# An HGRN2 and ConvFFN layer on one core: the modulation's column loads issued from GpSimd's queue

## The chip, the cores and the metric

One core of a Trainium2 chip runs the whole layer. The metric is the time of one execution on the device in microseconds (us). Engines are named by what they do and, in the rows, by the profile's short names: TensorE (PE; PEld for its weight loads), VectorE (DVE), ScalarE (ACT), GpSimd (POOL), SyncE (SP). Each runs its own queue of instructions strictly in order. A transfer (DMA) is issued from a queue, too, and waits there until what it overwrites has been read.

## The reference

One layer for 256 latent tokens (x) and 256 context tokens (ctx), 2048 wide, fp32. A vector c gives six rows of modulation for the latents (c_ctx for the context): shift, scale and gate of the mixer, shift, scale and gate of the FFN.

```
m = silu(c) @ ada_w + ada_b                 # (2048) x (2048 x 6*2048); parts 0 to 5
h = norm(x) * (1 + m[1]) + m[0]             # the context with silu(c_ctx)
y = hgrn2(h_latent, h_context)              # 16 heads: q, f, b, v, g = h @ w_in; gated recurrence, both ways
x = x + m[2] * norm(y)
h = norm(x) * (1 + m[4]) + m[3]
f = (silu(conv3(h @ w_gate)) * (h @ w_up)) @ ffn_w_out
out = x + m[5] * norm(f)
```

## The kernel before

Every weight comes from HBM as fp32, as a tile w_raw of 512 KB (L133, four buffers), and is split into a high and a low half: ScalarE casts w_hi (L108), VectorE subtracts and writes w_lo (L109). TensorE then makes three matmuls of each product (mm3, L212 to L214: high with high, high with low, low with high). w_hi and w_lo have three buffers; the casts run up to two tiles ahead (`LOOK`). A w_raw buffer is free for the next load when w_lo has been written.

The program runs in stages: the start (all tokens normalised; the first four heads, weights taken in rows of w_in), the projection of the heads in pairs p = 2 to 7 with the recurrence of earlier pairs (`scan`) laid between their matmuls, the mixer's output product, the FFN's input products (22 blocks), the FFN's output product.

Parts 0 and 1 of the modulation are made on TensorE at the start. Parts 2 to 5 are made by `ada_part` (L355), one column block at a time: a tile ada_w of 128 rows by 512 columns (256 KB) is loaded (L359), and VectorE multiplies it by a column of c and adds it up into ada_acc (L374 for the first of 16, L376 for the rest; here called *sums*). A part has 4 blocks of 16 tiles, so 64 loads and 64 sums; TensorE then adds the 128 partitions with a matrix of ones (L385). `loaded` is called ahead: ada_w has four buffers (`ADA_BUFS`), in part 5 five (`GATE_BUFS`), and each new load waits for the sum that read its buffer. Parts 2 to 4 are stepped along with the projection (`ada_rest`, `step`), part 5 along with the FFN's blocks. Parts 2 and 5 end with two memsets on GpSimd (L406), for the bias and the gain.

The order on each engine isn't written out: a scheduler puts the instructions into the queues by the program's priorities and by its own model of what is ready when. The weights' preparation has a raised priority (L138). SyncE's queue holds all loads, the weights' and these.

In `scan`, the output of a pair is squared on ScalarE (L843), VectorE makes 1/sqrt in small steps (`rsqrt`, L78 to L83), ScalarE scales by it (L850), and TensorE transposes the result (L858).

Of the kernel before, what the change touches and what calls it, by code (L numbers as in the profile page):

```python
# [17 lines left out]
P = 128  # L18
D = 2048
# [18 lines left out]
def tile_hgrn2_convffn_layer(  # L38
# [4 lines left out]
    nc = tc.nc  # L43
    V, S, PE = nc.vector, nc.scalar, nc.tensor
    x, ctx_in, out = x[0], ctx_in[0], out[0]
    ada_w, ada_b = ada_w[0], ada_b[0]
# [23 lines left out]
    def bank(pool, name):  # L70
        return pool.tile([P, 512], F32, name=name)
# [283 lines left out]
    def ada_part(part, pool, bufs=ADA_BUFS):  # L355
        def loaded(i):
            b, r = divmod(i, KT)
            aw = pool.tile([P, 512], F32, name="ada_w", bufs=bufs)
            nc.sync.dma_start(out=aw, in_=ada_w[r * P:(r + 1) * P, part * D + b * 512:part * D + (b + 1) * 512])  # L359
            return aw  # L360

        accs = []
        aws = [loaded(i) for i in range(bufs - 1)]
        yield
        yield
        for b in range(4):
            acc = pool.tile([P, 512], F32, name="ada_acc", bufs=4)
            for r in range(KT):

                if len(aws) < 4 * KT:  # L370
                    aws.append(loaded(len(aws)))
                aw = aws[b * KT + r]
                if r == 0:
                    V.tensor_scalar(out=acc, in0=aw, scalar1=c_cols[:, r:r + 1], scalar2=None, op0=ALU.mult)  # L374
                else:
                    V.scalar_tensor_tensor(out=acc, in0=aw, scalar=c_cols[:, r:r + 1], in1=acc,  # L376
                                           op0=ALU.mult, op1=ALU.add)
                yield
            accs.append(acc)
        for _ in range(8):  # L380
            yield

        one = bank(ps_mi, "mi")
        for b in range(4):
            PE.matmul(out=one[32 * b:32 * b + 32, :], lhsT=ones32, rhs=accs[b], start=True, stop=True,  # L385
                      tile_position=(0, 32 * b), skip_group_check=True)
        strip_sb = pool.tile([P, 512], F32, name="ada_w", bufs=bufs)
        S.copy(out=strip_sb, in_=one)
        for _ in range(4):
            yield  # L390
        if part in (3, 4):
            tp = bank(ps_mi, "mi")
            for i in range(4):
                PE.transpose(out=tp[:, i * P:(i + 1) * P], in_=strip_sb[:, i * P:(i + 1) * P], identity=ident)
            dst = shc_f if part == 3 else scc_f

            V.tensor_tensor(out=dst.rearrange("p (b i) -> p i b", i=4),
                            in0=tp.rearrange("p (i b r) -> p i b r", i=4, r=32)[:, :, :, 0],
                            in1=adab[:, part, :].rearrange("p (b i) -> p i b", i=4), op=ALU.add)
            if part == 4:  # L400
                V.scalar_tensor_tensor(out=scc_f, in0=scc_f, scalar=1.0, in1=g_ffn, op0=ALU.add, op1=ALU.mult)
        else:
            post = n_mix_post if part == 2 else n_ffn_post
            for w, src in enumerate((ada_b[part * D:(part + 1) * D], post[0])):
                gb = pool.tile([P, 512], F32, name="ada_acc", bufs=4)
                nc.gpsimd.memset(gb, 0.0)  # L406
                nc.sync.dma_start(out=gb[0::32, :], in_=src.rearrange("(b n) -> b n", b=4))
                V.tensor_tensor(out=strip_sb, in0=strip_sb, in1=gb, op=(ALU.add, ALU.mult)[w])
            gd = dram.tile([4, 512], F32, name=f"gd{part}")
            nc.sync.dma_start(out=gd, in_=strip_sb[0::32, :])  # L410
            grow[part] = gd
        yield
# [755 lines left out]
```

## Time and profile before

| | |
|---|---|
| median of 3 runs | 1739.77 us (1739.51 to 1744.2) |
| the profiled execution | 1737.13 us, its span 1735.4 us, mean granted clock 0.996 |
| TensorE busy | 1688.0 us (97%) |
| VectorE busy | 1154.8 us (67%) |
| ScalarE busy | 772.9 us (45%) |
| GpSimd busy | 3.4 us |
| read from HBM | 348 MB, 202 GB/s over the span |
| loads of ada_w | 256 of 256 KB, from SyncE's queue, median 4.1 us to landing |

The span runs from the first to the last instruction; the execution's own time lies 1.7 us around it. Busy time is a union: overlapping matmuls count once. A row of waiting names the instruction that waited, what ended the wait, the total in us, how often, and the longest. Issuing a transfer isn't counted as busy time.

### The profile page before, as it was taken

How to read it: one execution, taken by the hardware profiler on the slowest of the kernel's cores; microseconds unless marked ns; L12 is line 12 of the kernel's file. 1: busy time of each engine (PE TensorE's matmuls, PEld its weight loads, DVE VectorE, ACT ScalarE, POOL GpSimd, SP SyncE). 2: the span in 40 equal slices, each digit the busy share in tenths (PEclk: the TensorE clock that was granted, in tenths of full speed). 3: DMA queues.
4: the chain of work that ended last, by engine and by line, in shares of the span. 5: the costliest groups of instructions: out<-in, count | busy, mean ns of one | idle time of the engine just before them, and what ended most of it. 6: DMA issues, size and time to landing. Idle time of an engine off the chain costs nothing.

```text
span 1735.4 us, 31973 instructions
## 1 busy us (share of the span) xinstructions
PE 1688.0 (97%) x12990; PEld 1506.1 (87%) x12990; DVE 1154.8 (67%) x1857; ACT 772.9 (45%) x1176; POOL 3.4 (0%) x13
## 2 busy tenths in 40 slices
PE   6999999899999999999999899999999999999998
PEld 4777888888989899888988798999999999888886
DVE  6777898855548875697565798766666666544444
ACT  4322264454544354443464644444444444443443
POOL 0000000000000000000000000000000000000000
PEclk9999999999999999999999999999999999999999
DMA  9886657633326863677357579766666666655654
GB/s 353 289 299 231 223 171 233 216 108 107 110 75 204 287 213 106 206 235 231 111 166 271 192 262 314 235 193 194 190 195 195 194 194 195 202 195 192 199 194 146
DMA packets 274646, 352.57 MB, mean 203 GB/s; under 512 B 12954, under 2 KB 197675, under 8 KB 273987
## 3 DMA queue, kind: packets, MB, share of 16 engines
q1 hardware_dynamic: 274499, 350.53, 62.1%
q8 instruction: 102, 1.67, 0.4%
q14 instruction: 45, 0.37, 0.1%
HBM read 348.37 MB, written 2.11 MB: 202 GB/s over the span
## 4 chain that ended last, share of the span: by engine, by line
PE 78%; DVE 10%; DMA 8%; issue 3%; ACT 1%; SPq 0%; DVEq 0%; ACTq 0%
PE pj L212 24%; PE pj L214 24%; PE pj L213 24%; DMA ada_w<-in_ada_w_dram 7%; DVE ada_acc L376 3%; DVE w_lo L109 2%; PE o L429 2%; DVE k L706 1%; PE sc L746 1%; PE mi L818 1%; DMA aw<-in_ada_w_dram 0%; ACT w_hi L108 0%; PE pj L347 0%; DMA w_raw<-in_hgrn_w_in_dram 0%; DVE f L709 0%
## 5 line engine op out<-in xcount | busy, mean ns | idle before, releaser
L109 DVE TENSOR_TENSOR w_lo<-w_raw,w_hi 128x1024 fp32r<-128x1024 f32 x452 | 552.9, 1224 | 393.6 <-ACT w_hi L108 389.7
L108 ACT CAST w_hi<-w_raw 128x1024 fp32r<-128x1024 f32 x452 | 473.3, 1049 | 679.0 <-PE pj L213 369.6
L214 PE MATMUL pj<-h2h,w_lo 128*128 128x256 f32 x1376 | 380.9, 277 | 5.4 <-DVE w_lo L109 5.3
L212 PE MATMUL pj<-h2h,w_hi 128*128 128x256 f32 x1376 | 380.2, 276 | 0.0
L213 PE MATMUL pj<-h2l,w_hi 128*128 128x256 f32 x1376 | 379.9, 276 | 0.0
L212 PE MATMUL pj<-hTh,w_hi 128*128 128x256 f32 (+1 forms) x1040 | 352.9, 340 | 2.7 <-ACT hTh L108 1.6
L214 PE MATMUL pj<-hTh,w_lo 128*128 128x256 f32 (+1 forms) x1040 | 347.6, 335 | 0.8 <-DVE w_lo L109 0.6
L213 PE MATMUL pj<-hTl,w_hi 128*128 128x256 f32 (+1 forms) x1040 | 347.3, 334 | 0.0
L214 PEld LDWEIGHTS pj<-h2h,w_lo 128*128 128x128 f32 x1376 | 258.3, 188 | 6.9 <-DVE w_lo L109 6.8
L212 PEld LDWEIGHTS pj<-h2h,w_hi 128*128 128x128 f32 x1376 | 258.3, 188 | 0.9 <-issue 0.8
L213 PEld LDWEIGHTS pj<-h2l,w_hi 128*128 128x128 f32 x1376 | 258.3, 188 | 0.0
L212 PEld LDWEIGHTS pj<-hTh,w_hi 128*128 128x128 f32 x1040 | 195.5, 188 | 31.1 <-issue 5.0
L214 PEld LDWEIGHTS pj<-hTh,w_lo 128*128 128x128 f32 x1040 | 195.3, 188 | 23.8 <-DVE w_lo L109 2.1
L213 PEld LDWEIGHTS pj<-hTl,w_hi 128*128 128x128 f32 x1040 | 195.7, 188 | 19.6 <-DVE hTl L109 0.2
L376 DVE SCALAR_TENSOR_TENSOR ada_acc<-ada_w,c_cols,ada_acc 128x512 f32<-128x512 f32 x240 | 179.8, 750 | 45.2 <-DMA ada_w<-in_ada_w_dram 42.0
L214 PE MATMUL pj<-w_hi,al 128*128 128x512 f32 x352 | 138.7, 394 | 0.0
L213 PE MATMUL pj<-w_lo,ah 128*128 128x512 f32 x352 | 138.0, 392 | 0.0
L212 PE MATMUL pj<-w_hi,hTh 128*128 128x256 f32 (+1 forms) x448 | 135.3, 302 | 1.5 <-DVE q L481 0.8
L212 PE MATMUL pj<-w_hi,ah 128*128 128x512 f32 x352 | 136.6, 388 | 0.0
L213 PE MATMUL pj<-w_lo,hTh 128*128 128x256 f32 (+1 forms) x448 | 133.0, 297 | 0.2 <-DVE w_lo L109 0.2
L214 PE MATMUL pj<-w_hi,hTl 128*128 128x256 f32 (+1 forms) x448 | 133.1, 297 | 0.0
L212 PEld LDWEIGHTS pj<-w_hi,hTh 128*128 128x128 f32 x448 | 85.3, 190 | 5.7 <-DVE stage L479 1.7
(227 smaller groups left out, 1792.8 us busy)
## 6 DMA issues: line engine op xcount, KB each, us to landing
w_raw<-in_ffn_w_in_dram SPq DMA_DIRECT2D x172, 512.0 KB, 3.6
w_raw<-in_hgrn_w_in_dram SPq DMA_DIRECT2D x160, 512.0 KB, 4.5
ada_w<-in_ada_w_dram SPq DMA_DIRECT2D x256, 256.0 KB, 4.1
w_raw<-in_ffn_w_out_dram SPq DMA_DIRECT2D x88, 512.0 KB, 4.0
aw<-in_ada_w_dram SPq DMA_DIRECT2D x64, 512.0 KB, 8.0
w_raw<-in_hgrn_w_out_dram SPq DMA_DIRECT2D x32, 512.0 KB, 4.3
hTh<-in_x_dram SPq DMA_DIRECT2D x2, 1024.0 KB, 4.9
hTh<-in_ctx_dram SPq DMA_DIRECT2D x2, 1024.0 KB, 10.2
```

What stands on the lines that cost most here:

```text
L108: S.copy(out=hi, in_=src)
L109: V.tensor_tensor(out=lo, in0=src, in1=hi.bitcast(F32), op=ALU.subtract)
L212: PE.matmul(out=o, lhsT=lh, rhs=rh, start=first, stop=False, skip_group_check=True)
L213: PE.matmul(out=o, lhsT=lh, rhs=rl, start=False, stop=False, skip_group_check=True)
L214: PE.matmul(out=o, lhsT=ll, rhs=rh, start=False, stop=last, skip_group_check=True)
L376: V.scalar_tensor_tensor(out=acc, in0=aw, scalar=c_cols[:, r:r + 1], in1=acc, op0=ALU.mult, op1=ALU.add)
L429: PE.matmul(out=strip[32 * a:32 * (a + 1), :], lhsT=cst[:, r4 * 4 + a, :], rhs=aws[r4][:, a].rearrange("p s n -> p (s n)"), start=(r4 == 0 ...
L706: V.tensor_tensor(out=half(t, i, m), in0=half(t, i, m), in1=half(by, 1 - i, m)[:, :, 0:1].to_broadcast([P, 256 // m, m]), op=ALU.mult)
L746: PE.matmul(out=o[32 * b:32 * b + 32, 32 * i:32 * i + 32], lhsT=flat(lhs[b % 2])[:, s0:s0 + 32], rhs=flat(rhs[b % 2])[:, t0:t0 + 32], star ...
L818: PE.matmul(out=sps[:, cs], lhsT=kT[:, d, h, ct], rhs=v[:, 2 + ct, h * P:(h + 1) * P], start=(ct == 0), stop=(ct == 1))
```

## The change

The loads of L359 are issued from GpSimd's queue. Nothing else is edited.

```
-            nc.sync.dma_start(out=aw, in_=ada_w[r * P:(r + 1) * P, part * D + b * 512:part * D + (b + 1) * 512])
+            nc.gpsimd.dma_start(out=aw, in_=ada_w[r * P:(r + 1) * P, part * D + b * 512:part * D + (b + 1) * 512])
```

The scheduler builds other orders from it. GpSimd's queue, from the end of the start on; the memsets are those of parts 2 and 5 (ident and ib are constants):

```order
 L320 IOTA ib 128x32
-L406 MEMSET ada_acc 128x512 x4
+L359 DMA ada_w<-in_ada_w_dram 128x512 x64
+L406 MEMSET ada_acc 128x512 x2
+L359 DMA ada_w<-in_ada_w_dram 128x512 x192
+L406 MEMSET ada_acc 128x512 x2
```

All 256 loads now stand there, with two memsets between the loads of part 2 and those of part 3; SyncE's queue keeps the rest in the order it had.

VectorE in part 4, from the row that ends part 3 (L397 writes shc_f) on, before:

```order
L397 TENSOR_TENSOR shc_f<-mi,colsB 128x4x4
L376 SCALAR_TENSOR_TENSOR ada_acc<-ada_w,c_cols,ada_acc 128x512 x5
L109 TENSOR_TENSOR w_lo<-w_raw,w_hi 128x1024
L376 SCALAR_TENSOR_TENSOR ada_acc<-ada_w,c_cols,ada_acc 128x512 x4
L109 TENSOR_TENSOR w_lo<-w_raw,w_hi 128x1024
L376 SCALAR_TENSOR_TENSOR ada_acc<-ada_w,c_cols,ada_acc 128x512 x5
L109 TENSOR_TENSOR w_lo<-w_raw,w_hi 128x1024
L374 TENSOR_SCALAR ada_acc<-ada_w,c_cols 128x512
L376 SCALAR_TENSOR_TENSOR ada_acc<-ada_w,c_cols,ada_acc 128x512 x2
L109 TENSOR_TENSOR w_lo<-w_raw,w_hi 128x1024
L376 SCALAR_TENSOR_TENSOR ada_acc<-ada_w,c_cols,ada_acc 128x512
L109 TENSOR_TENSOR w_lo<-w_raw,w_hi 128x1024
```

The same place now:

```order
L397 TENSOR_TENSOR shc_f<-mi,colsB 128x4x4
L376 SCALAR_TENSOR_TENSOR ada_acc<-ada_w,c_cols,ada_acc 128x512 x6
L109 TENSOR_TENSOR w_lo<-w_raw,w_hi 128x1024
L376 SCALAR_TENSOR_TENSOR ada_acc<-ada_w,c_cols,ada_acc 128x512 x5
L109 TENSOR_TENSOR w_lo<-w_raw,w_hi 128x1024
L376 SCALAR_TENSOR_TENSOR ada_acc<-ada_w,c_cols,ada_acc 128x512
L374 TENSOR_SCALAR ada_acc<-ada_w,c_cols 128x512
L376 SCALAR_TENSOR_TENSOR ada_acc<-ada_w,c_cols,ada_acc 128x512 x4
L109 TENSOR_TENSOR w_lo<-w_raw,w_hi 128x1024
L376 SCALAR_TENSOR_TENSOR ada_acc<-ada_w,c_cols,ada_acc 128x512 x2
L109 TENSOR_TENSOR w_lo<-w_raw,w_hi 128x1024
L376 SCALAR_TENSOR_TENSOR ada_acc<-ada_w,c_cols,ada_acc 128x512 x3
```

Ahead of the third w_lo stand 17 sums of this piece where 14 stood, ahead of the fifth 22 where 18 stood; one more sum has moved to just ahead of the piece.

VectorE in part 2, at the end of the rsqrt of the first pair (rs and nw_t are its tiles; L650 gates the q of pair 3 and L689 begins the next recurrence), before:

```order
L376 SCALAR_TENSOR_TENSOR ada_acc<-ada_w,c_cols,ada_acc 128x512
L109 TENSOR_TENSOR w_lo<-w_raw,w_hi 128x1024
L82 TENSOR_TENSOR nw_t_2921<-nw_t_2921,ss_2912 128x4
L376 SCALAR_TENSOR_TENSOR ada_acc<-ada_w,c_cols,ada_acc 128x512
L83 SCALAR_TENSOR_TENSOR rs_2913<-nw_t_2921,rs_2913 128x4
L109 TENSOR_TENSOR w_lo<-w_raw,w_hi 128x1024
L689 TENSOR_TENSOR tmp<-k_3128,k_3133 128x512
```

and now:

```order
L376 SCALAR_TENSOR_TENSOR ada_acc<-ada_w,c_cols,ada_acc 128x512
L109 TENSOR_TENSOR w_lo<-w_raw,w_hi 128x1024
L82 TENSOR_TENSOR nw_t_2921<-nw_t_2921,ss_2912 128x4
L650 SCALAR_TENSOR_TENSOR q<-pj,tmp 128x512
L83 SCALAR_TENSOR_TENSOR rs_2913<-nw_t_2921,rs_2913 128x4
L689 TENSOR_TENSOR tmp<-k_3128,k_3133 128x512
```

The w_lo that followed the last L83 is now ahead of it (it is the one shown), and so are L650 and, counted from the start of the burst, two more sums. On TensorE the four transposes L858 of this pair stand 22 matmuls later than before; its order is otherwise the same.

## Rows read from the trace of the kernel before

**Rows 1.** Page of the profile: span, and busy us (share) xinstructions by engine.

```profile
span 1735.4 us, 31973 instructions
...
PE 1688.0 (97%) x12990; PEld 1506.1 (87%) x12990; DVE 1154.8 (67%) x1857; ACT 772.9 (45%) x1176; POOL 3.4 (0%) x13
```

**Rows 2.** Who waited for whom, TensorE, whole run: us in total, times, longest.

```profile
PE pj L214 <- DVE w_lo L109: 5.9, 9, 1.9
PE mi L858 <- ACT tmp L850: 5.8, 2, 4.3
```

**Rows 3.** Stretches: the four bursts and one without; us, each engine's busy us (instructions), clock, DMA.

```profile
core 0: us, PE busy (x) PEld busy (x) DVE busy (x) ACT busy (x) POOL busy (x), PEclk, DMA share, GB/s
262.00:352.00 90.00, 85.23 (x900) 76.76 (x899) 79.28 (x165) 42.57 (x89) 0.00 (x0) 0.96 0.68 217
529.00:632.00 103.00, 100.90 (x878) 90.89 (x877) 91.41 (x164) 43.89 (x81) 0.00 (x0) 1.00 0.79 254
705.00:815.00 110.00, 105.17 (x901) 94.25 (x901) 90.22 (x162) 43.41 (x82) 0.00 (x0) 1.00 0.75 240
1014.00:1102.00 88.00, 82.57 (x709) 81.06 (x708) 78.91 (x103) 39.60 (x47) 0.00 (x0) 1.00 0.90 302
1115.00:1203.00 88.00, 88.00 (x778) 88.00 (x778) 54.51 (x61) 42.42 (x49) 0.00 (x0) 1.00 0.62 192
```

**Rows 4.** Tile ada_w in each burst: idle before its instructions until what; us, times.

```profile
  DMA ada_w<-in_ada_w_dram: 8.1, 7
...
  DMA ada_w<-in_ada_w_dram: 10.6, 14
...
  DMA ada_w<-in_ada_w_dram: 15.9, 13
...
  DMA ada_w<-in_ada_w_dram: 8.9, 10
```

**Rows 5.** Tile ada_w, whole run: duration ns min/median/max; landing us.

```profile
L359 SPq DMA_DIRECT2D ada_w<-in_ada_w_dram x256: 327/328/1370, 204.6 to 1091.2; - x128
...
L374 DVE TENSOR_SCALAR ada_acc<-ada_w,c_cols x16: 460/480/488, 210.6 to 1069.2; 128x512 f32<-128x512 f32 x16
...
DMA to landing us min/median/max: 2.5/4.1/6.3
```

**Rows 6.** VectorE in order of time, part 4: start us, us, instruction [idle before].

```profile
718.55 0.75 DVE L376 SCALAR_TENSOR_TENSOR ada_acc<-ada_w,c_cols,ada_acc 128x512 f32<-128x512 f32 x1 [2.67 <-DMA ada_w<-in_ada_w_dram]
...
726.45 3.12 DVE L376 SCALAR_TENSOR_TENSOR ada_acc<-ada_w,c_cols,ada_acc 128x512 f32<-128x512 f32 x4 [1.85 <-DMA ada_w<-in_ada_w_dram]
731.44 0.75 DVE L376 SCALAR_TENSOR_TENSOR ada_acc<-ada_w,c_cols,ada_acc 128x512 f32<-128x512 f32 x1 [1.87 <-DMA ada_w<-in_ada_w_dram]
732.11 1.22 DVE L109 TENSOR_TENSOR w_lo<-w_raw,w_hi 128x1024 fp32r<-128x1024 f32 x1
```

**Rows 7.** Who waited for whom, SyncE's queue, whole run.

```profile
SPq L133 <- DVE w_lo L109: 862.6, 352, 8.5
...
SPq L359 <- DVE ada_acc L376: 96.5, 142, 5.8
```

**Rows 8.** VectorE in order of time, FFN burst.

```profile
1034.02 0.75 DVE L376 SCALAR_TENSOR_TENSOR ada_acc<-ada_w,c_cols,ada_acc 128x512 f32<-128x512 f32 x1
```

**Rows 9.** SyncE's queue in order of time, FFN burst.

```profile
1038.48 0.38 SPq L133 DMA_DIRECT2D w_raw<-in_ffn_w_in_dram  x1
1038.90 0.51 SPq L359 DMA_DIRECT2D ada_w<-in_ada_w_dram  x1
```

**Rows 10.** GpSimd in order of time, around the end of part 2.

```profile
526.73 0.99 POOL L406 MEMSET ada_acc<- 128x512 f32 x2 [524.79 <-PE mi L385]
```

**Rows 11.** TensorE in order of time, part 4.

```profile
733.38 0.39 PE L214 MATMUL pj<-hTh,w_lo 128*128 128x256 f32 x1 [0.21 <-DVE w_lo L109]
```

**Rows 12.** Stretches behind TensorE's wait of 4.3 us, columns as in rows 3.

```profile
318.70:323.10 4.40, 4.40 (x21) 4.40 (x22) 3.67 (x8) 3.19 (x11) 0.00 (x0) 0.50 1.00 342
323.10:327.50 4.40, 4.40 (x41) 4.40 (x41) 3.29 (x9) 1.78 (x4) 0.00 (x0) 1.00 0.06 22
```

## Prediction

> **What bounds the kernel now.** I read the engines' busy time first, then who waits for whom, then the four stretches in which the moved loads run, and last the order of the instructions in them.
>
> TensorE is busy for 1688 us of a span of 1735.4, VectorE for 1155 [rows 1]. So whatever the change does, it can give back only what TensorE waits for, 47 us in all. Its longer waits behind VectorE's in-order queue are 5.9 us for w_lo (the low halves of the weights), and 5.8 us for the transposes of L858, which wait for ScalarE's L850, which waits for the last step of VectorE's rsqrt [rows 2].
>
> The 256 moved loads fall into four bursts of 64, one for each part: three while the pairs of heads are projected, one at the start of the FFN. In the four TensorE idles 4.8, 2.1, 4.8 and 5.4 us, VectorE 11, 12, 20 and 9; in the FFN's burst TensorE runs 709 matmuls in 88 us where the same length of time without a burst takes 778, so that burst costs 69/778 of 88 us = 7.8 us of TensorE [rows 3].
>
> VectorE's own waits in the bursts are for these loads: 7, 14, 13 and 10 of them, 8.1 to 15.9 us in each [rows 4]. A burst has four buffers (the FFN's five). A load is issued when the sum four places ahead has read its buffer, and it lands 4.1 us (median; least 2.5) after that [rows 5]. A buffer's round in the projection is thus about 0.33 issue + 4.1 landing [rows 5] + 0.78 for the sum itself (3.12 us for four [rows 6]) = 5.2 us, with the semaphores between them about 5.3, so four buffers give a sum each 1.33 us where VectorE alone would take 0.78. **The round trip of one load sets the pace of a burst**, not the bytes: the DMA engines are 75 to 79% busy in parts 3 and 4, and 90% in the FFN's burst [rows 3].
>
> Last, the queue that is relieved. SyncE's weight loads wait for VectorE's w_lo, which gives their buffer back (352 waits, 863 us), and its ada_w loads wait for the sums, 97 us [rows 7]. Neither wait is the other's fault while the pairs are projected. In the FFN it is: the sum that ends at 1034.8 (0.75 after 1034.02) frees a buffer, but the load for it is issued at 1038.90, behind a weight load that waited until 1038.48 for w_lo [rows 8, 9]. That is 4.1 us of queue. This is what the change can win.
>
> **The change, part by part.**
>
> *SyncE* loses 256 issues of 0.33 us [rows 5], 84 us of a queue that nobody is waiting on. Worth 0 by itself: its weight loads wait for VectorE's w_lo [rows 7], not for the queue. The Trainium skill, "DMA: Bandwidth & Descriptors", section "Issuing engines are not separate DMA queues", says that loads from all queues run on the same 16 engines and that a second queue saves only the issuing time. By that rule alone the sum would be 0; the traces' head-of-line wait above and VectorE's new order below are what it leaves out. It is my second case.
>
> *GpSimd* gets 256 loads and is otherwise idle. Queued on it beside them are only the four memsets of L406; the first two now stand between part 2's loads and part 3's, and take 0.99 us together at 526.7 [rows 10]. The first loads of part 3 go out some 3 us later than now, at a place where TensorE waits for no w_lo. Cost 0.
>
> *FFN burst (part 5).* Loads no longer wait behind weights: up to 4.1 us off a round. VectorE's 10 waits there are 8.9 us [rows 4], TensorE's loss 7.8. But the DMA engines are at 90% [rows 3]: of 88 us only 10% is left. Bounds 0 and -7.8. I take **-3.5**, a little under half, since the freed loads press on the same nearly full engines.
>
> *VectorE's order.* The scheduler now places the sums earlier, ahead of w_lo that TensorE is about to need. In part 4 the third w_lo after shc_f has 18 sums of the burst before it where it had 14, the fifth 23 where it had 18 (one of the extra ones stands just ahead of the piece shown). The third w_lo runs at 732.11 and TensorE is waiting for it: its matmul starts at 733.38 after a wait [rows 6, 11]. So all that is put ahead of it goes to TensorE: four sums at 0.78 (data there) to 1.33 (paced by the round trip), 3.1 to 5.3 us, up to 6.6 with the fifth's. Three waits for landings, of 2.7, 1.9 and 1.9 us, stand right ahead of it [rows 6], so I take the pace: **+5.3**. In part 2 the last rsqrt step has two more sums, one w_lo and one L650 before it: 2 x 0.78 to 2 x 1.33, plus 1.2 and some 0.6 = 3.4 to 4.5 us later. TensorE comes to the four transposes 22 matmuls of 0.107 us (4.4 / 41 [rows 12]) = 2.4 us later. Net +1.0 to +2.1, taken **+1.3**; the wait of 4.3 us stays that long, and so the clock still falls with it: after the wait TensorE runs at 0.50 (1.2 GHz) for 4.4 us, 21 matmuls where the next 4.4 us have 41 [rows 12]. In part 3 one sum more stands ahead of most w_lo: 0 where TensorE has reserve, 1.3 where not, taken **+0.6**. Sum +7.2.
>
> *The round trip.* No load in the trace is issued by GpSimd, so the change of a load's round, d, has to be bounded. From below: if a queue of its own spares a load all waiting behind weights, it lands in the least time, 2.5 instead of 4.1 [rows 5]: d = -1.6. From above: GpSimd has to make up the transfer itself, and takes 0.5 us for one pass over a tile of this shape (two in 0.99 [rows 10]); one pass for the reading and one for the writing side, against 0.33 issue, make +0.7 (2 x 0.5 - 0.33), and SyncE's slowest issue, 1.37 us [rows 5], +1.0. I take **d = +0.4**, between one pass (+0.2) and two (+0.7), and so near the upper end, because half of the waiting behind weights is not saved when two queues share the engines. The Trainium skill ("DMA: Bandwidth & Descriptors", "Latency and other measured facts") gives about 1 us to the first byte from GpSimd and 0.6 from SyncE; by that alone d would be +0.4 too, and no run here shows it yet. Of the 34 waits in parts 2 to 4 [rows 4] I count about half, 16, ahead of places where TensorE has no reserve; the rest falls into VectorE's other idle time. 16 x 0.4 = **+6.4**.
>
> Sum: -3.5 + 7.2 + 6.4 = **+10.1 us**. The profiled execution took 1737.1, so 1747.2; the runs shown have a median of 1739.8, 2.7 above it, so **1749.9 us**, 0.6% slower.
>
> **The rivals.**
>
> *No change.* GpSimd's loads land as SyncE's did, and the sums put earlier are covered by time that VectorE would have idled. For it: VectorE idles 9 to 20 us in each burst [rows 3]. Against: at the tight places it idles for these loads alone. With d = 0 the sum is 7.2 - 3.5 = +3.7, 1743.5.
>
> *Faster.* A load no longer stands behind 512 KB of weights, neither in SyncE's queue nor in the DMA engines' rings. For it: the landings of 4 to 6 us beside a least of 2.5. It decides from d about -0.6. At d = -0.8 the 16 waits give back 12.8, but in the projection TensorE has no more to give than the waits of L858 and w_lo and the slow clock behind one of them, about 4.3 + 2.2 [rows 2, 12] + 1 = 7.5; VectorE's order then costs only 0.78 a sum, 3.1 + 0.8; the FFN gives 6: -9.6, 1730.
>
> *GpSimd as the pace.* If a load takes GpSimd more than the 1.33 us of a round's quarter, the queue itself sets the bursts. At 2 us, 64 loads take 128 us where the bursts take 88 to 110 [rows 3]: some 17 us of TensorE in each of four after reserves of about 10, near 1807. The Trainium skill ("SBUF — State Buffer", "SBUF: two separate sides") describes such a trap: GpSimd cannot write a load's descriptors while VectorE holds their shared port. It names copies and single-input operations in a fast mode, and here that is 16 sums of 0.48 us [rows 5] of 256; the rest have two inputs. So I give it little.
>
> *It doesn't take effect* is excluded: GpSimd's queue holds the 256 loads in the built order.
>
> **How the numbers follow.** Forecast (d from 0.1 to 1): 0.50. No change: 0.26. Faster: 0.14. GpSimd as the pace: 0.10. About 0.3%, 5.2 us, is what a measurement of this kernel can tell from no change; the forecast and the last case lie above it, so slower 0.60, same 0.26, faster 0.14. Range: upward all terms at their worse end short of the last case, 6.6 + 2.1 + 1.3 + 0 and d = 0.7 in all 34 waits (24) = +33, 1773; downward into the faster case as far as 1735. What is left out is most of the last case and the better part of the faster one, about 0.17.
>
> **What would show it.** After: the loads stand under a second queue; the issue-to-landing median is 4.2 to 4.8 us; VectorE's waits for ada_w grow from 45 to 55 us or more; TensorE waits for w_lo near the third w_lo of part 4, several us, instead of 0.21; the FFN's burst has more than 709 matmuls in its 88 us. I am wrong if the landings come down to 3.5 us or less, if TensorE's waits for w_lo in parts 2 to 4 stay under 2 us, or if the FFN's burst gains more than 6 us.

## The result, and the profile after

| | before | changed |
|---|---|---|
| median of 3 runs | 1739.77 us | 1758.76 us (1756.33 to 1761.8) |
| ratio | | 1.0109, 95% interval 1.0091 to 1.0128 |
| span of the profiled execution | 1735.4 us | 1760.0 us |

The change costs 19.0 us, 1.1%. The forecast was +10.1 us (1749.9, range 1735 to 1773): the right side and inside the range, but little more than half the size.

The page of the changed kernel's profile, span and busy time (before: [rows 1]):

```profile
span 1760.0 us, 32088 instructions
...
PE 1699.7 (97%) x12990; PEld 1518.3 (86%) x12990; DVE 1154.8 (66%) x1857; ACT 773.1 (44%) x1176; POOL 140.7 (8%) x269
```

The 24.6 us of longer span fall in two parts. TensorE is idle for 60.3 us instead of 47.4, 12.9 more. And it is *busy* for 11.7 us more with the same 12990 matmuls: that is a lower clock, as the rows on the clock below show. VectorE's busy time is the same to the tenth, so no work was added there.

Who waited for whom, TensorE, whole run (before: [rows 2]):

```profile
PE mi L858 <- ACT tmp L850: 12.6, 2, 8.2
PE pj L214 <- DVE w_lo L109: 9.6, 7, 4.0
```

The transposes L858 wait 12.6 us instead of 5.8, the matmuls behind w_lo 9.6 instead of 5.9. The four bursts, in windows that begin and end at the same instructions of TensorE (to within a few) as those of [rows 3], and the stretch without a burst; columns as there:

```profile
263.70:359.90 96.20, 87.88 (x900) 79.26 (x899) 80.75 (x167) 42.62 (x89) 25.19 (x47) 0.95 0.65 208
537.00:649.30 112.30, 102.60 (x878) 92.18 (x877) 91.17 (x164) 43.63 (x81) 34.48 (x65) 0.95 0.77 247
722.10:840.40 118.30, 109.81 (x901) 98.84 (x900) 92.83 (x165) 46.70 (x85) 32.70 (x61) 0.96 0.70 226
1040.50:1126.60 86.10, 82.79 (x705) 81.81 (x705) 79.85 (x104) 39.95 (x46) 23.14 (x43) 0.98 0.94 314
1139.60:1227.60 88.00, 88.00 (x779) 88.00 (x778) 54.50 (x61) 42.39 (x49) 0.00 (x0) 1.00 0.63 193
```

For the same matmuls part 2 now takes 96.2 us instead of 90, part 3 112.3 instead of 103, part 4 118.3 instead of 110. The FFN's burst has 705 matmuls in 86.1 us, 720 in 88, where it had 709. Without a burst nothing changed. The clock column (PEclk) was 0.96 in part 2 and 1.00 in the other bursts; it is now between 0.95 and 0.98 in all four.

Tile ada_w, whole run: duration of the issue in ns, landing in us (before: [rows 5]):

```profile
L359 POOL DMA_DIRECT2D ada_w<-in_ada_w_dram x256: 536/536/676, 207.8 to 1107.6; - x128
...
DMA to landing us min/median/max: 2.8/3.9/6.5
```

GpSimd takes 0.54 us for a load (SyncE: 0.33), never over 0.68, and it lands 3.9 us after its issue (4.1).

Where two of the longest stalls come from can be read on VectorE and TensorE. Part 3, the rsqrt before the second L858 (the row of L844 begins it, the last L83 ends it; time, us, instruction, idle before):

```profile
612.99 0.16 DVE L844 TENSOR_SCALAR ss<-ss 128x4 f32<-128x4 f32 x1
613.11 0.75 DVE L376 SCALAR_TENSOR_TENSOR ada_acc<-ada_w,c_cols,ada_acc 128x512 f32<-128x512 f32 x1
...
616.90 0.75 DVE L376 SCALAR_TENSOR_TENSOR ada_acc<-ada_w,c_cols,ada_acc 128x512 f32<-128x512 f32 x1 [1.58 <-DMA ada_w<-in_ada_w_dram]
...
618.43 0.48 DVE L374 TENSOR_SCALAR ada_acc<-ada_w,c_cols 128x512 f32<-128x512 f32 x1
...
620.57 0.75 DVE L376 SCALAR_TENSOR_TENSOR ada_acc<-ada_w,c_cols,ada_acc 128x512 f32<-128x512 f32 x1 [1.20 <-DMA ada_w<-in_ada_w_dram]
621.24 1.22 DVE L109 TENSOR_TENSOR w_lo<-w_raw,w_hi 128x1024 fp32r<-128x1024 f32 x1
622.37 0.15 DVE L83 SCALAR_TENSOR_TENSOR rs<-nw_t,rs 128x4 f32<-128x4 f32 x1
```

The same place in the trace of before:

```profile
601.27 0.16 DVE L844 TENSOR_SCALAR ss<-ss 128x4 f32<-128x4 f32 x1
...
606.20 0.15 DVE L83 SCALAR_TENSOR_TENSOR rs<-nw_t,rs 128x4 f32<-128x4 f32 x1
```

From L844 to the end of the last L83 it took 5.1 us and now takes 9.5: one sum, an L374 and a w_lo more stand in between (0.75 + 0.48 + 1.22 = 2.4 us), and two loads are waited for (1.58 + 1.20). TensorE, in order of time, in part 3 and at the third w_lo of part 4 (there 0.21 before [rows 11]):

```profile
622.98 0.73 PE L858 MATMUL mi<-ident,tmp 128*128 128x128 f32 x2 [8.24 <-ACT tmp L850]
...
754.71 0.58 PE L214 MATMUL pj<-hTh,w_lo 128*128 128x256 f32 x1 [3.99 <-DVE w_lo L109]
```

And the clock around the first of them, two stretches of equal length (columns as in [rows 3]):

```profile
616.70:627.00 10.30, 4.02 (x12) 3.13 (x12) 8.80 (x19) 3.11 (x6) 4.28 (x8) 0.50 0.68 227
627.00:637.30 10.30, 10.30 (x46) 8.35 (x45) 7.90 (x11) 1.82 (x2) 3.75 (x7) 1.00 0.76 248
```

The clock is at its lower level, 1.2 GHz (0.50), for 10.3 us that begin within the wait, and back at 1.00 after it.

VectorE in part 4, ahead of the third w_lo, the one that TensorE waits 3.99 us for (before: [rows 6]):

```profile
735.19 2.37 DVE L376 SCALAR_TENSOR_TENSOR ada_acc<-ada_w,c_cols,ada_acc 128x512 f32<-128x512 f32 x3 [3.31 <-DMA ada_w<-in_ada_w_dram]
...
744.74 0.75 DVE L376 SCALAR_TENSOR_TENSOR ada_acc<-ada_w,c_cols,ada_acc 128x512 f32<-128x512 f32 x1 [2.09 <-DMA ada_w<-in_ada_w_dram]
...
751.98 1.54 DVE L376 SCALAR_TENSOR_TENSOR ada_acc<-ada_w,c_cols,ada_acc 128x512 f32<-128x512 f32 x2 [2.49 <-DMA ada_w<-in_ada_w_dram]
753.43 1.22 DVE L109 TENSOR_TENSOR w_lo<-w_raw,w_hi 128x1024 fp32r<-128x1024 f32 x1
```

**By stage.** For the rest of the document the loss is counted by stages: the start of the same TensorE instruction, counted from the first, in two traces, and by how much its lag grows from one end of a stage to the other. (Instructions number 1530, 2428, 3999, 4874, 5605, 6505, 7684 and 8663 start at 262, 352, 529, 632, 705, 815, 985 and 1115 us in the trace of before.) Elsewhere little is lost after the start. One trace is one execution: the profiled one of before is 2.7 us below its median, so lags count from a low mark. How far a single stage can be trusted shows in e3: up to the FFN its orders and queues are those of before, and its stages still differ by up to 1.6 us. The last column compares medians, each with runs of the kernel before taken beside it (1738.39 to 1740.32 us).

| us against the trace of before | part 2 | part 3 | part 4 | FFN burst | elsewhere | median against before |
|---|---|---|---|---|---|---|
| changed kernel | +6.2 | +9.3 | +8.3 | -1.8 | +2.7 | +19.0 |
| changed kernel again (e4) | +3.4 | +11.0 | +6.0 | -0.8 | +1.3 | +17.3 |
| GpSimd's queue, old order (e1) | +3.6 | +6.9 | -2.0 | -5.7 | +1.5 | +1.4 |
| SyncE's queue, new order (e2) | +3.2 | +5.8 | +5.1 | +4.3 | +2.4 | +17.5 |
| only the FFN's loads on GpSimd (e3) | +1.6 | +0.6 | -1.0 | -1.1 | -0.2 | -4.4 |
| changed kernel, rsqrt in one piece (e5) | +1.5 | +7.2 | +5.8 | +0.2 | +0.2 | +15.3 |
| new order to part 3, then old (e6) | +5.0 | +12.2 | -2.3 | -5.4 | -0.4 | +5.9 |
| old order, slower loads (e7) | +7.8 | +19.2 | +9.4 | -1.3 | +2.3 | +34.4 |
| FFN's loads on GpSimd, rsqrt in one piece (e8) | +0.4 | -0.6 | -1.8 | -2.1 | +2.6 | -2.3 |
| sums tied, GpSimd's queue (e9) | -6.9 | -3.3 | -5.8 | -6.6 | +0.6 | -22.9 |
| sums tied, SyncE's queue (e10) | -6.9 | -3.3 | -4.8 | -7.9 | +1.1 | -22.8 |
| sums tied, GpSimd's queue, slower loads (e11) | -6.9 | -3.0 | -5.1 | -7.8 | 0.0 | -23.4 |

### The profile page after: what moved, and what is told of

It reads as the page before. It is cut to its first block, busy times and chain, and to the rows that moved or that the text cites. A ratio compares the mean times of both kernels' runs of the same rounds, so it can differ in the third digit from the quotient of the medians.

```text
span 1760.0 us, 32088 instructions
## 1 busy us (share of the span) xinstructions
PE 1699.7 (97%) x12990; PEld 1518.3 (86%) x12990; DVE 1154.8 (66%) x1857; ACT 773.1 (44%) x1176; POOL 140.7 (8%) x269
## 4 chain that ended last, share of the span: by engine, by line
PE 75%; issue 9%; DMA 7%; DVE 5%; POOL 2%; ACT 1%; SPq 0%; POOLq 0%; DVEq 0%; ACTq 0%
PE pj L212 23%; PE pj L214 23%; PE pj L213 23%; DMA ada_w<-in_ada_w_dram 7%; POOL ada_w L359 2%; PE o L429 2%; DVE ada_acc L376 1%; DVE w_lo L109 1%; PE sc L746 1%; PE mi L818 1%; DMA aw<-in_ada_w_dram 0%; ACT w_hi L108 0%; DMA w_raw<-in_hgrn_w_in_dram 0%; DVE k L706 0%; PE pj L347 0%
## 5 line engine op out<-in xcount | busy, mean ns | idle before, releaser
L212 PE MATMUL pj<-hTh,w_hi 128*128 128x256 f32 (+1 forms) x1040 | 356.6, 344 | 4.1 <-ACT w_hi L108 2.5
L359 POOL DMA_DIRECT2D ada_w<-in_ada_w_dram x256 | 137.4, 537 | 779.8 <-DVE ada_acc L376 207.8
```

Source lines behind the costliest of these rows:

```text
L212: PE.matmul(out=o, lhsT=lh, rhs=rh, start=first, stop=False, skip_group_check=True)
L359: nc.gpsimd.dma_start(out=aw, in_=ada_w[r * P:(r + 1) * P, part * D + b * 512:part * D + (b + 1) * 512])
```

## Experiments

In e1, e2 and e5 to e8 the engines' orders are written out: the instructions of an engine, by name, are chained in the wanted order by edges that fix the order and add no wait.

```
+    for packed in ORDERS:
+        names = ["I-%d" % n for n in json.loads(zlib.decompress(base64.b64decode(packed)))]
...
+        for a, b in zip(names, names[1:]):
+            tc.add_manual_dep(traced[b], a, mybir.DependencyInfo(mybir.DependencyClass.NoSync, mybir.DependencyReason.DATA), reason="order")
```

### e1: GpSimd's queue, the old order

The changed kernel with the edges above, for VectorE and ScalarE as they stood before the change.

> GpSimd issues all 256 loads, but VectorE's and ScalarE's instructions stand in the order that they had before the change (the order is written out; TensorE's comes out the same too). Theory A, the order: the loss of parts 2 to 4 comes from the sums that the scheduler now puts ahead of w_lo and of the rsqrt steps, so with the old order it goes: within 5 us of the kernel before, the stall of L858 in part 3 is back at 1 to 2 us, the third w_lo of part 4 waits under 0.5 us, and the stages from 260 to 830 us lose under 4 us where they lost 23. Theory B, the queue: a load issued by GpSimd begins about 0.3 us later and is made up in 0.54, and the weights share the engines with it, so the loss stays: +15 us or more. The prediction's own split (order +7.2, round trip +6.4, FFN -3.5) would give +2.9.

Measured: 1741.56 us, ratio 1.0018 (0.9999 to 1.0037), +1.4 us by the medians (12 runs from 1737.76 to 1758.0), which is not clear of no change. So the queue alone does not make the loss. By stage it is not nothing: it costs 3.6 and 6.9 us in parts 2 and 3 and gives 2.0 in part 4 and 5.7 in the FFN. L858 in part 3 waits 1.93 us, as theory A has it, but the projection's stages lose 8.5 us in sum, not under 4: theory B has a share there, which the FFN's gain hides in the total.

### e2: SyncE's queue, the new order

The kernel before with the edges, for VectorE, ScalarE and TensorE in the order that the change gave them.

> SyncE issues all loads as before the change, but VectorE's, ScalarE's and TensorE's instructions stand in the order that the change gave them (written out). Theory A, the order: most of the loss is here without GpSimd's queue: +12 to +22 us, with L858 in part 3 waiting 5 us or more and w_lo at the third place of part 4 some 3 to 5 us. Theory B, the queue: within 5 us of the kernel before. The prediction's split would give +7.2.

Measured: 1757.66 us, ratio 1.0100 (1.0083 to 1.0117), +17.5 us with no load on GpSimd. TensorE in order of time, the same two places:

```profile
616.94 0.99 PE L858 MATMUL mi<-ident,tmp 128*128 128x128 f32 x3 [6.98 <-ACT tmp L850]
...
746.53 0.57 PE L214 MATMUL pj<-hTh,w_lo 128*128 128x256 f32 x1 [3.09 <-DVE w_lo L109]
```

Theory A holds: the order alone makes nearly the whole loss, and makes both long waits. It costs in the FFN, too, 4.3 us. There TensorE waited for w_lo, before:

```profile
PE pj L214 <- DVE w_lo L109: 5.3, 6, 1.9
```

and here, with the new order from SyncE:

```profile
PE pj L214 <- DVE w_lo L109: 7.6, 8, 2.1
```

With the old order from GpSimd (e1) it is 1.1 us. Order and queue by themselves, 17.5 and 1.4 us, add up to 18.9; the change costs 19.0, and 17.3 when measured again (e4).

### e3: only the FFN's loads on GpSimd

```
-            nc.sync.dma_start(out=aw, in_=ada_w[r * P:(r + 1) * P, part * D + b * 512:part * D + (b + 1) * 512])
+            (nc.gpsimd if part == 5 else nc.sync).dma_start(out=aw, in_=ada_w[r * P:(r + 1) * P, part * D + b * 512:part * D + (b + 1) * 512])
```

Within the FFN's burst VectorE's order is the one that it has in the changed kernel.

> Only part 5's 64 loads go to GpSimd; parts 2 to 4 stay with SyncE, and every engine's order up to the FFN is that of before. By theory A and B alike the 23 us between 260 and 830 us go, and what is left is the FFN's burst by itself: the trace of the change lost 3 us there on the way and had 0.7 us less delay behind it than ahead of it, so -1 us, between -4 and +1. The prediction's term was -3.5.

Measured: 1735.75 us, ratio 0.9975 (0.9963 to 0.9987), -4.4 us. This part of the change is a gain, between 2.3 and 6.4 us by the interval, and somewhat larger than the trace of the change had led me to expect. The one trace of it doesn't show where the gain lies: it has -1.1 us in the FFN's burst and the same span as the trace of before.

### e4: the changed kernel again

> The changed kernel itself, on the same chip as the three others, for a second trace. If the 2.6 us lost before 70 us, where no moved load has been issued yet and the program is the same, belong to one execution, this trace loses under 1 us there; if they stay, something of the program's start differs. The rest should repeat within 3 us: about 5 us in part 2, 9 in part 3, 8 in part 4, -1 in the FFN.

Measured: 1757.37 us, ratio 1.0104 (1.0076 to 1.0133). It loses nothing before 70 us, so the 2.6 us there belonged to one execution. The stages repeat, with up to 2.8 us of scatter in one of them.

### e5: the rsqrt in one piece

The changed kernel with its own orders written out, but in parts 2 and 3 the steps L78 to L83 that stood among sums follow L844 directly (VectorE, part 2, cut):

```
 L844 TENSOR_SCALAR ss_2912<-ss_2912 128x4
-L376 SCALAR_TENSOR_TENSOR ada_acc<-ada_w,c_cols,ada_acc 128x512
 L78 TENSOR_SCALAR nw_j_2920<-ss_2912 128x4
-L376 SCALAR_TENSOR_TENSOR ada_acc<-ada_w,c_cols,ada_acc 128x512
 L79 TENSOR_SCALAR rs_2913<-nw_j_2920 128x4
...
+L83 SCALAR_TENSOR_TENSOR rs_2913<-nw_t_2921,rs_2913 128x4
+L376 SCALAR_TENSOR_TENSOR ada_acc<-ada_w,c_cols,ada_acc 128x512 x3
+L109 TENSOR_TENSOR w_lo<-w_raw,w_hi 128x1024
```

> The changed kernel with its own orders written out, but for one thing: the steps of rsqrt (L78 to L83) that stand among sums, in two places of parts 2 and 3, follow each other right behind L844; the sums and w_lo that stood between them come after. If the sums inside the rsqrt make the loss of part 3 (L858 waits 8.2 us, and TensorE's clock is low around it), the chain there ends some 7 us earlier, L858 waits under 2 us, and the kernel comes down by 8 to 13 us from the 1757 to 1759 of the change, to 1745 to 1750. Rival: the sums are only late somewhere else, for w_lo that now stands behind all of them, or the pace of GpSimd's loads decides: under 3 us gained.

Measured: 1755.59 us, ratio 1.0078 (1.0061 to 1.0095): some 2 to 3 us better than the change, not 8 to 13; the intervals overlap, so even that is not clear of none. Part 3 still loses 7.2 us (9.3 and 11.0 in the two traces of the change). The wait of L858 is gone altogether, but who waited for whom now reads, for TensorE:

```profile
PE pj L214 <- DVE w_lo L109: 16.3, 14, 3.7
```

That was 9.6 us in the changed kernel (10.4 in e4). My expectation failed and its rival came true: the sums that stood in the rsqrt now stand ahead of w_lo, wait for their loads there, and TensorE waits for w_lo instead.

### e6: the old order from part 4 on

The changed kernel with the change's order on VectorE up to the row that ends part 3 (L397), from there on the old one.

> The changed kernel, with the change's order on VectorE up to the row that ends part 3 (L397) and the old order from there on (part 4, FFN); all loads from GpSimd. If the sums ahead of the third w_lo of part 4 make that part's loss, as the prediction had it, the 6 to 8 us between 705 and 815 us go, TensorE's wait at that w_lo with them, and the FFN gives 4 to 5.6 us as it did with the old order: -8 to -13 us from the change, 1745 to 1750. Rival, the queue: the stage goes on losing 5 us or more.

Measured: 1746.17 us, ratio 1.0023 (1.001 to 1.0036), 11 to 13 us less than the change. Part 4 goes from +8.3 to -2.3 us. All that TensorE waits for there, from 723 to 833 us, is

```profile
PE o L837 <- DVE tmp L825: 1.3, 1, 1.3
PE sc L783 <- DVE QA L706: 0.7, 1, 0.7
```

and no w_lo at all. The loss of part 4 was the order, with GpSimd's queue unchanged. In the FFN the old order brings -5.4 us where the changed kernel has -1.8.

### e7: each load half a microsecond slower, old order

e1 (with TensorE's order written out as well) and one instruction more on GpSimd for each load:

```
-            aw = pool.tile([P, 512], F32, name="ada_w", bufs=bufs)
+            aw = pool.tile([P, 512], F32, name="ada_w", bufs=bufs); nc.gpsimd.memset(aw, 0.0)
```

> GpSimd issues all loads, VectorE, ScalarE and TensorE stand in the old order, and ahead of each load GpSimd clears the buffer (a memset of 128x512, about 0.5 us by the trace), so each load's round is 0.5 to 0.6 us longer than in the run with the old order alone (1741.6). The prediction priced a round at 16 exposed waits: +8 to +10, about 1750; if every one of some 45 waits counts, +25; if the round is covered and only the order matters, under +3.

Measured: 1774.67 us, ratio 1.0188 (1.0168 to 1.0207), 33 us more than e1: worse than the upper case. But a load is late by more than the memset's 0.53 us, since GpSimd sits idle between a memset and the issue behind it, 113 times and 0.30 us each (tile ada_w, idle until what; us, times):

```profile
  POOL ada_w L358: 33.5, 113
```

From the sum that frees a buffer to the landing of its next load the median is 0.75 to 1.03 us longer than in e1, by part. At that, every one of some 45 waits would give 34 to 46 us, an estimate from these two numbers. VectorE's waits for loads in the burst of part 3, before:

```profile
DVE ada_acc L376 <- DMA ada_w<-in_ada_w_dram: 9.0, 12, 1.9
DVE ada_acc L374 <- DMA ada_w<-in_ada_w_dram: 1.6, 2, 1.3
```

and here:

```profile
DVE ada_acc L376 <- DMA ada_w<-in_ada_w_dram: 23.1, 19, 3.6
DVE ada_acc L374 <- DMA ada_w<-in_ada_w_dram: 8.3, 3, 4.4
```

VectorE waits 20.8 us more, and TensorE loses 19.2. The other bursts read alike: part 2 from 8.1 to 16.1 us of waits, TensorE +7.8; part 4 from 15.9 to 23.6, TensorE +9.4. In e1 the waits change by +4.1, +7.7, -3.6 and, in the FFN, -6.4 us, TensorE by +3.6, +6.9, -2.0 and -5.7. **As long as VectorE's order stays the same, what it waits more in a burst is passed on to TensorE nearly one to one**, its low clock included.

### e8: the FFN's loads on GpSimd and the rsqrt in one piece

e3 with the edit of e5, in the three places where rsqrt steps stood among sums.

> Only part 5's loads on GpSimd (1735.75), and the rsqrt steps that stand among sums follow each other right behind L844, as in the other run; the rest of the order as it was. There L858 waits 7.2 us in 2 places (5.1 the longest), with 3.7 us at the low clock behind it. If the sums inside the rsqrt make these waits too, -5 to -9 us: 1727 to 1731. If w_lo behind the sums is late instead, no change.

Measured: 1738.0 us, ratio 0.9983 (0.9968 to 0.9997): nothing gained on e3 (the intervals overlap). L858's 7.2 us are gone and w_lo's waits grow from 4.5 to 7.3. A miss, for the reason of e5.

### e9, e10, e11: sums that don't run ahead

If the bursts are the cause, the cure is to have none. Each sum is tied behind the w_lo that had last been written in the program when the sum was, by an edge for the order on VectorE alone, so that only a few sums stand between two w_lo (VectorE's own order, no waits between engines; TensorE's, VectorE's and ScalarE's orders are the same for both queues):

```
-        V.tensor_tensor(out=lo, in0=src, in1=hi.bitcast(F32), op=ALU.subtract)
+        return V.tensor_tensor(out=lo, in0=src, in1=hi.bitcast(F32), op=ALU.subtract)
...
-                split(hi, lo, self.raw[i])
+                newest[0] = split(hi, lo, self.raw[i])
...
-                    V.scalar_tensor_tensor(out=acc, in0=aw, scalar=c_cols[:, r:r + 1], in1=acc,
+                    one = V.scalar_tensor_tensor(out=acc, in0=aw, scalar=c_cols[:, r:r + 1], in1=acc,
...
+                tc.add_manual_dep(one.ins, newest[0].ins.name, mybir.DependencyInfo(mybir.DependencyClass.NoSync, mybir.DependencyReason.DATA), reason="spread"); yield
```

e9 issues the loads from GpSimd:

> The changed kernel, but each sum is tied behind the w_lo last prepared when it was written (an edge for the order on VectorE alone, no wait between engines), so the sums can't run ahead in bursts: at most a few stand between two w_lo. If the loss is that of sums put ahead of w_lo and rsqrt while their loads are not there, it goes, and so do the waits of that kind that the kernel before has: TensorE waits under 2 us for w_lo in all and under 2 at L858, and the time is 1722 to 1732. Rival: GpSimd's loads cost by themselves (0.54 us each, sharing the engines with the weights): 1745 or more.

e10 from SyncE:

> The same tie of the sums, all loads from SyncE; TensorE's, VectorE's and ScalarE's orders are those of the run with GpSimd's queue. If a load's round is covered once the sums do not run in bursts, the two differ by under 2 us. If SyncE's queue holds loads up behind weights in the FFN as in the kernel before, this one is 3 to 5 us slower; if GpSimd's issuing costs by itself, it is faster by 5 or more.

e11 is e9 with the memset of e7:

> The run with the tie and GpSimd's queue, and a memset of the buffer (about 0.5 us) ahead of each load, which cost 33 us with the old order in bursts. If that was so dear because VectorE waits for each load in a burst, it costs under 4 us here; if GpSimd's memset costs in another way (a port, the DMA engines), 15 us or more here too.

| | median | ratio (95%) |
|---|---|---|
| e9, GpSimd | 1715.45 us | 0.9872 (0.9852 to 0.9891) |
| e10, SyncE | 1715.58 us | 0.9872 (0.9850 to 0.9895) |
| e11, GpSimd, slower loads | 1715.01 us | 0.9869 (0.9850 to 0.9888) |

All three beat both kernels, by 23 us the one before and 43 the changed one, more than the 6 to 16 expected. And the queue, which was at issue, is worth 0.1 us, within the scatter; the memset that cost 33 us in bursts costs nothing. Page of e9, and VectorE's waits for loads in the whole run:

```profile
span 1713.4 us, 32066 instructions
...
PE 1682.1 (98%) x12990; PEld 1504.8 (88%) x12990; DVE 1153.8 (67%) x1857; ACT 776.2 (45%) x1176; POOL 140.6 (8%) x269
```

```profile
DVE ada_acc L376 <- DMA ada_w<-in_ada_w_dram: 4.9, 7, 1.0
```

VectorE does the same work in 1153.8 us. TensorE waits 0.2 us for w_lo in the whole run and not at all at L858, as expected. TensorE's busy time has come down from 1688.0 to 1682.1 us, its idle time from 47.4 to 31.3. The loads themselves land as before, e9:

```profile
DMA to landing us min/median/max: 2.8/4.1/6.0
```

and e10:

```profile
DMA to landing us min/median/max: 2.6/3.7/5.9
```

Part 2's sums now run from 354 to 495 us, where they ran from 211 to 352, and no loss shows there. GpSimd's loads are 0.4 us later, and that costs nothing that the times show. (The trace of e10 records only 68 of its 256 landings; over the same 68 loads e9's median is 4.0 us.)

## Why the prediction was right, and where it was too small

**The side, and the mechanism.** The forecast was slower by two terms of nearly one size: VectorE's new order, which puts sums that wait for loads ahead of what TensorE needs, and a longer round for each load. The first holds: e2 shows that the order by itself, on three engines, costs 17.5 us with the old queue, and e6 that in part 4 it is VectorE's. The time lay in the range.

**FFN, -3.5: near, but with a term left out.** Timed by itself (e3) it is -4.4 us, while the stages have -1.8 in the changed kernel, -0.8 in e4 and -1.1 in e3. They are the sum of two things: the queue gives 5.7 us with the old order (e1; 5.4 in e6), and the new order takes 4.3 (e2). The forecast had nothing for the order in the FFN. That -3.5 came out near is in part luck. The head-of-line wait was real: from the sum that frees a buffer to the landing of its next load it took a median of 7.3 us before (over the 24 loads whose landing is recorded) and takes 5.0 in the changed kernel. The upper bound I gave, that the DMA engines have only 10% left, did not bite: they went from 90 to 94%.

**VectorE's order, +7.2: the term that was mis-sized.** By the stages of e2 it is 3.2 + 5.8 + 5.1 = 14.1 us in parts 2 to 4, and the FFN's 4.3 come on top.
- Part 4, +5.3: right (5.1). The pace of 1.33 us a sum was a little high: the landing's 4.1 us count from the start of the issue, so the 0.33 us of the issue were counted twice. Without them it is 1.2 us, and four sums are 4.9. The third w_lo was the place, with a wait of 3.99 us instead of 0.21, and e6 took it away.
- Part 2, +1.3: 3.2. The wait of L858 stays at 4.38 us, as I had it; but in the changed kernel a wait of 2.3 us for w_lo at 315.7 and a slow stretch came on top (in e2 that wait is 2.5 us). The difference is hardly more than two traces of one program differ by.
- **Part 3, +0.6: 5.8** from the order alone, 9 to 11 with the queue. This is the step that failed. I counted there only the sums ahead of w_lo and did not read how the order had changed inside the rsqrt, though I had read exactly that in part 2. In part 3 the rsqrt had almost no wait behind it (TensorE 1.5 us), so there was no stall to see in the trace of before; there was also no reserve. Reading it would have named the place, not the cure: without the sums inside the rsqrt (e5) part 3 still loses 7.2 us, since TensorE then waits for w_lo.

**The round trip, +6.4: right in sum, wrong in its working.** e1 gives 3.6 + 6.9 - 2.0 = 8.5 us in parts 2 to 4. I had d = +0.4 us on 16 of 34 waits. From the freeing sum to the landing the median went from 3.37 to 3.89 us in part 2, from 4.14 to 4.09 in part 3 and from 4.35 to 4.24 in part 4 (before and e1, over the recorded landings, 21 to 23 of 60 in a part before and all in e1): d is mostly smaller. But not half of the waits counts; all of VectorE's waiting does (e7). Two errors cancelled. Why VectorE waits more in part 3 and less in part 4 from the same queue is not settled: which loads meet a 512 KB weight on the engines was not taken apart.

**The clock** I had counted once, behind the L858 of part 2. In the changed kernel's trace nine stretches run at the lower level where two did before. TensorE is busy for 33.8 us in them (7.4 before); half of the difference, 13.2 us, is an estimate of their cost. By the page its busy time is 11.7 us longer, of 24.6 us of longer span. Two of the nine lie before 70 us, where no moved load has been issued. In e4's trace, which has none there, TensorE's busy time is 7.0 us longer (1695.0 against 1688.0), of 20.9 us of longer span. So a forecast of waits alone leaves out about a third of their price.

**What would show it.** Of the five signs three came: the second queue, the wait at the third w_lo, the FFN's matmuls (720 in 88 us). Two did not: the landing's median is 3.9, not 4.2 to 4.8, and VectorE's waits for ada_w went from 45 to 48.7 us in all, not to 55. The loss came with hardly more waiting on VectorE, because the waits had moved to where TensorE has no reserve.

**The rivals.** *No change* had in its favour that all queues feed the same engines, which the Trainium skill says ("DMA: Bandwidth & Descriptors", "Issuing engines are not separate DMA queues"). e9 and e10 agree with it, 1715.45 and 1715.58 us; in bursts it left out the wait behind weights in one queue (e3: -4.4 us). GpSimd's loads land 0.4 us later in e9 than SyncE's in e10 (4.1 and 3.7 us). The Trainium skill's two latencies to the first byte, about 1 and 0.6 us ("DMA: Bandwidth & Descriptors", "Latency and other measured facts"), differ by as much. But with the order of before, GpSimd's (e1) land in 3.9 us and SyncE's (before) in 4.1, over the 98 loads that both traces record, so no run here shows that this latency is the cause. *GpSimd as the pace* did not occur: 0.68 us is its longest issue. But e7, where GpSimd spends 0.54 + 0.53 us on a load and is busy for 65.4 of the 116.6 us of part 3's burst, shows that the bursts get dear long before the queue is full.

## What to carry to other kernels

- Where a scheduler orders the queues, an edit of one load's queue is an edit of every engine's order. Separate the two before judging either: old order with the new queue, new order with the old queue. Here the order was +17.5 us and the queue +1.4, and within that the queue cost 8.5 us in parts 2 to 4 and gave 5.7 in the FFN.
- Work that nobody needs soon (these sums) must not be let ahead of what the bottleneck needs next, however idle the engine looks. Shifting the late instruction (e5, e8) only chose another that was late; tying each sum to its place in the program gave 23 us and made the queue irrelevant.
- Read the order at every chain that ends at the bottleneck, also where the trace before shows no wait: no wait can mean no reserve.

## What was unexpected of the hardware

In bursts paced by their loads, a memset of 0.53 us ahead of each load made a round 0.75 to 1.03 us longer and the kernel 33 us slower, 0.13 us for each of the 256 loads; with the sums tied to their places the same memset cost nothing (e11). And TensorE's clock: in the changed kernel stalls of 1.6 to 8.2 us came with stretches of 3.4 to 10.2 us at 1.2 GHz, so that the matmuls themselves took 11.7 us longer, about as much as the added waiting (12.9 us). In e9, with waits for w_lo and L858 gone, one such stretch is left before the end, at 973 us, in the step between the mixer and the FFN.
